# Attention values in plain float32: one matmul in place of three, one copy in place of a split

## The chip, the cores and the metric

The kernel runs as one program on one core of a Trainium2 chip. Its time is the device time in microseconds of that core. Three runs of the kernel before gave 996.60, 995.01 and 995.56 us, a median of 995.56. A further execution was taken with the hardware profiler; all the rows below are from it.

## The reference, cut to what matters

The reference is one encoder layer on 512 tokens of width 1024, in float32: a half-step gated feed-forward network, a mixing block with two groups of eight attention heads, a second half-step feed-forward network and a final norm. The change touches the mixing block alone:

```
qa, ka = rmsnorm(...), rmsnorm(...)          # group A: 8 heads of 64
va = proj[..., o_va:o_cq]
p  = softmax(qa ka^T * scale + bias, masked) # 64-token chunks, block-causal
out_a = p @ va
...
q, k = [nope 64 | rotary 32]                 # group B: 8 heads, 96 wide
v  = kv[..., B_NOPE:]
p  = softmax(q k^T * scale, masked)
out_b = p @ v
x = x + concat(out_a, out_b) @ w_out
```

With 512 tokens, each 128-query block sees the keys up to its own block, so of the 4 x 4 blocks of a head's probabilities ten are computed.

## The kernel before, in words

Everything is kept transposed or split so that the tensor engine (PE) does nearly all the work. A float32 operand is split in two float32r parts, a high part (a rounding copy, mostly on the scalar engine, ACT) and a low part (what is left, on the vector engine, DVE, or on GpSimd, POOL). A product is then three float32r matmuls: high x high, high x low, low x high. The helper `mm3` at lines 146 to 149 issues them, so in the profile L147, L148 and L149 are the three products of every matrix multiply, and the tiles' names tell which one it is. Weights come in units of up to 1024 columns through `wunit` (L139 load, L142 high part, L143 low part) with four buffers each for the raw, high and low tiles (tags `raw`, `whi`, `wlo`).

The stages follow each other in time: first feed-forward network (up to about 362 us), the mixing block (362 to 579 us), output projection (`wo`, from 579 us) and the second feed-forward network. The order of instructions on each engine is set by a scheduler when the program is built, from the order of the code and its own estimates, and each engine then runs its queue in that order. Only the very end has an order written out by hand.

In the mixing block `in_proj` gives A's queries, keys and values; the latents give B's queries (`uq`) and B's keys and values (`ukv`, L414). B's values are evacuated from `ukv` into VBh and VBl (L426, L427). GpSimd squares B's keys (`sqk`, L420), DVE sums them (`ssk`), and their norm factors (`f_kn`) follow. It also applies B's rotary embedding to the queries (lines 294 to 304). A's keys need their own norm factors: squares on ACT (`sqp`, L330), sums on DVE (`ss_ka`, L331), the reciprocal root (`f_ka`, lines 114 to 119 and 288), and a multiply (kA, L375). A's values come last (`values_proj`, VAh and VAl). The value tiles are 192 columns wide for each pair of heads: values of the even head, 64 zeros, values of the odd head. A 128-column window of it as the stationary operand puts one head in its half of the output rows and adds zeros to the other half, so a pair of heads accumulates into one bank `pv`.

The loop over 16 heads runs four steps on different heads: `front` makes the transposed query and key operands, `softmax` makes the four row blocks of probabilities (scores `s`, minimum and mask on DVE at L522, exponential on ACT at L524, reciprocal on DVE, scaling on GpSimd at L526), `flip` transposes the ten 128 x 128 blocks on PE into three banks t0, t1, t2 (L542) and copies them out, and `values` multiplies them with the values into `pv`. Heads 0 to 7 are group A, with a contraction of 64 rows in the scores; heads 8 to 15 are group B, with 96 rows.

In `flip`, the transposed probabilities for keys in block 0, 1, 2 and 3 have 512, 384, 256 and 128 query columns. Block 3 is widened with 128 zero columns to 256 (the GpSimd memsets at L544). Each of the four pieces is copied as a high part by ACT (L547), then DVE subtracts that from the bank for the low part (L548). `values` then issues four times three matmuls, with 512, 384, 256 and 256 columns.

Of the kernel before, what the change touches and what calls it, by code (L numbers as in the profile page):

```python
# [10 lines left out]
F32 = mybir.dt.float32  # L11
F32R = mybir.dt.float32r
# [5 lines left out]
P = 128  # L18
# [21 lines left out]
def tile_macaron_block(  # L40
# [207 lines left out]
    with tc.tile_pool(name="mix", bufs=1, side="left", reuse_waits="tile") as mp:  # L248
        latT = mp.tile([P, 6, S], F32R, tag="vAh", name="latT")
        VBh = mp.tile([P, NT, 4, 192], F32R, tag="vBh", name="VBh")  # L250
        qA = mp.tile([P, NT, 512], F32, tag="qA", name="qA")
        VBl = mp.tile([P, NT, 4, 192], F32R, tag="vBl", name="VBl")
# [4 lines left out]
        for t in (VBh, VBl):  # L257
            pool.memset(t[:, :, :, HD:2 * HD].bitcast(F32), 0.0)
# [47 lines left out]
        with tc.tile_pool(name="ps2", bufs=1, space=PSUM, reuse_waits="tile") as ps:  # L306
# [102 lines left out]
            for t in range(NT):  # L409
                tt = slice(t * P, (t + 1) * P)  # L410
                for half in range(2):
# [10 lines left out]
                    for e in range(2):  # L422
                        vh = VBh[:, t, 2 * half:2 * half + 2, 2 * HD * e:2 * HD * e + HD]
                        vl = VBl[:, t, 2 * half:2 * half + 2, 2 * HD * e:2 * HD * e + HD]
                        src = pv[:, e::2, HD:2 * HD]
                        act.copy(vh, src)  # L426
                        dve.tensor_tensor(out=vl, in0=src, in1=vh.bitcast(F32), op=ALU.subtract)  # L427
# [8 lines left out]
            def values_proj():  # L436

                VAh = mp.tile([P, NT, 4, 192], F32R, tag="vAh", name="VAh")
                VAl = mp.tile([P, NT, 4, 192], F32R, tag="vAl", name="VAl")
                for t in (VAh, VAl):  # L440
                    pool.memset(t[:, :, :, HD:2 * HD].bitcast(F32), 0.0)
                pts = in_proj(416 + 1024, 512, 1)
                for t in range(NT):
                    pv = pts[t].rearrange("p (h e w) -> p h e w", e=2, w=HD)
                    for e in range(2):
                        vh = VAh[:, t, :, 2 * HD * e:2 * HD * e + HD]
                        vl = VAl[:, t, :, 2 * HD * e:2 * HD * e + HD]
                        act.activation(vh, pv[:, :, e, :], AF.Copy, scale=rtok[:, t:t + 1])
                        dve.scalar_tensor_tensor(out=vl, in0=pv[:, :, e, :], scalar=rtok[:, t:t + 1], in1=vh.bitcast(F32),
                                                 op0=ALU.mult, op1=ALU.subtract)  # L450
                return VAh, VAl
# [77 lines left out]
            def flip(pi):  # L529
# [4 lines left out]
                PAh = wpool.tile([P, 1024], F32R, tag="whi", name="PAh")  # L534
                PAl = wpool.tile([P, 1024], F32R, tag="wlo", name="PAl")
                PBh = wpool.tile([P, 1024], F32R, tag="whi", name="PBh")
# [204 lines left out]
```

## Time and profile before

| what | value |
|---|---|
| median of three runs | 995.56 us |
| time of the profiled execution | 997.57 us |
| its span | 995.8 us |
| mean granted PE clock | 0.994 of full speed |
| PE busy | 975.5 us, 98% of the span |
| DVE, ACT, POOL busy | 390.5, 391.9, 579.6 us |
| the 16 heads | about 473 to 579 us |

The profiled execution took 997.57 us, of which 995.8 lie between its first and its last instruction; the remaining 1.8 us are around it. A busy time is the sum over the stretch in which an engine had an instruction running. Matmuls are pipelined: the next starts before the one before has ended, so a record's length (0.39 us for 512 columns) is longer than the distance from one start to the next, and the distance is what a matmul costs in a dense stream.

### The profile page before, as it was taken

Reading aid. Unit: us, or ns where it says so; the run is one execution under the profiler, and the core shown is the slowest. Engines: PE = TensorE matmul, PEld = TensorE weight load, DVE = VectorE, ACT = ScalarE, POOL = GpSimd, SP = SyncE. Lnnn points to the kernel's source line nnn. Section 1 sums busy time; section 2 is a strip of 40 time slices with the busy share of each in tenths; the row PEclk is TensorE's granted clock in tenths of the full one; section 3 lists DMA queues with packets and bytes.
Section 4 is the critical chain, followed back from the end, with each engine's and each line's share of the span. In section 5 each row is a group of like instructions: output and inputs, shape, how many; then the busy total and the mean of one; then the engine's idle time right before and its main releaser. Section 6 shows DMA issues by size and latency. Waiting matters only on the chain.

```text
span 995.8 us, 12076 instructions
## 1 busy us (share of the span) xinstructions
PE 975.5 (98%) x4579; PEld 812.1 (82%) x4579; DVE 390.5 (39%) x684; ACT 391.9 (39%) x661; POOL 579.6 (58%) x424
## 2 busy tenths in 40 slices
PE   9999999999999999898999999999999999999996
PEld 6888888888888889786778978888888888888886
DVE  7533333333121233866788845143333333200002
ACT  7533323232222236563778853343233232322321
POOL 4776666765555530385445567587666667645541
PEclk9999999999999999999999999999999999999998
DMA  6432223233233242220110062323322232333302
GB/s 233 145 109 86 102 89 106 85 106 95 83 102 93 89 141 75 85 64 1 32 33 2 1 212 88 103 86 106 102 88 99 93 104 80 101 96 95 101 16 85
DMA packets 29146, 89.90 MB, mean 90 GB/s; under 512 B 3488, under 2 KB 5664, under 8 KB 29088
## 3 DMA queue, kind: packets, MB, share of 16 engines
q1 hardware_dynamic: 28224, 88.34, 27.6%
q8 instruction: 36, 0.59, 0.2%
q10 hardware_dynamic: 864, 0.79, 0.2%
q14 instruction: 22, 0.18, 0.1%
HBM read 87.02 MB, written 2.10 MB: 89 GB/s over the span
## 4 chain that ended last, share of the span: by engine, by line
PE 89%; DVE 4%; ACT 3%; POOL 2%; issue 1%; DMA 1%; SPq 0%; POOLq 0%; ACTq 0%; DVEq 0%
PE gu L147 15%; PE gu L149 15%; PE gu L148 15%; PE dn L147 8%; PE dn L149 8%; PE dn L148 8%; PE pj L149 2%; PE pj L147 2%; PE pj L148 2%; PE wo L147 1%; PE wo L149 1%; PE wo L148 1%; PE t L542 1%; PE s L147 1%; PE tr L457 1%
## 5 line engine op out<-in xcount | busy, mean ns | idle before, releaser
L143 POOL TENSOR_TENSOR wlo<-raw,whi 128x1024 fp32r<-128x1024 f32 x138 | 324.2, 2350 | 153.3 <-ACT whi L142 152.5
L142 ACT CAST whi<-raw 128x1024 fp32r<-128x1024 f32 (+2 forms) x159 | 162.4, 1022 | 447.7 <-PE gu L148 244.8
L147 PE MATMUL gu<-x2h,whi 128*128 128x512 f32 x352 | 136.9, 389 | 0.0
L148 PE MATMUL gu<-x2l,whi 128*128 128x512 f32 x352 | 136.8, 389 | 0.0
L149 PE MATMUL gu<-x2h,wlo 128*128 128x512 f32 x352 | 136.8, 389 | 0.0
L148 PE MATMUL gu<-xl,whi 128*128 128x512 f32 x320 | 124.5, 389 | 0.0
L147 PE MATMUL gu<-xh,whi 128*128 128x512 f32 x320 | 124.5, 389 | 0.0
L149 PE MATMUL gu<-xh,wlo 128*128 128x512 f32 x320 | 124.5, 389 | 0.0
L162 POOL TENSOR_TENSOR us<-us,gs 128x512 f32<-128x512 f32 x44 | 57.6, 1310 | 108.7 <-DVE us L160 107.2
L161 DVE SCALAR_TENSOR_TENSOR gs<-th,gs 128x512 f32<-128x512 f32 x44 | 91.1, 2074 | 31.8 <-ACT th L159 31.8
L158 DVE TENSOR_TENSOR gs<-gu,rs 128x512 f32<-128x512 f32 x44 | 30.4, 691 | 175.9 <-PE gu L149 168.7
L191 DVE SCALAR_TENSOR_TENSOR x<-dn,x 128x512 f32<-128x512 f32 (+1 forms) x17 | 11.2, 660 | 193.9 <-PE dn L149 193.9
L148 PEld LDWEIGHTS gu<-x2l,whi 128*128 128x128 f32 x352 | 66.1, 188 | 13.8
L149 PEld LDWEIGHTS gu<-x2h,wlo 128*128 128x128 f32 x352 | 66.1, 188 | 13.8
L147 PEld LDWEIGHTS gu<-x2h,whi 128*128 128x128 f32 x352 | 66.1, 188 | 13.6
L149 PEld LDWEIGHTS gu<-xh,wlo 128*128 128x128 f32 x320 | 60.1, 188 | 12.6
L147 PEld LDWEIGHTS gu<-xh,whi 128*128 128x128 f32 x320 | 60.1, 188 | 12.5
L148 PEld LDWEIGHTS gu<-xl,whi 128*128 128x128 f32 x320 | 60.1, 188 | 12.3
L147 PE MATMUL dn<-h1h,whi 128*128 128x512 f32 x176 | 68.5, 389 | 0.0
L148 PE MATMUL dn<-h1l,whi 128*128 128x512 f32 x176 | 68.5, 389 | 0.0
L149 PE MATMUL dn<-h1h,wlo 128*128 128x512 f32 x176 | 68.5, 389 | 0.0
L160 DVE SCALAR_TENSOR_TENSOR us<-gu,rs 128x512 f32<-128x512 f32 x44 | 30.4, 690 | 64.9 <-PE gu L149 64.9
(327 smaller groups left out, 1864.5 us busy)
## 6 DMA issues: line engine op xcount, KB each, us to landing
raw<-in_gu SPq DMA_DIRECT2D x84, 512.0 KB, 3.6
raw<-in_dn SPq DMA_DIRECT2D x32, 512.0 KB, 3.5
raw<-in_dn SPq DMA_DIRECT2D x16, 384.0 KB, 3.1
raw<-in_w_in SPq DMA_DIRECT2D x12, 512.0 KB, 3.4
raw<-in_w_out SPq DMA_DIRECT2D x8, 512.0 KB, 4.3
x<-in_xT SPq DMA_DIRECT2D x8, 256.0 KB, 5.4
raw<-in_gu SPq DMA_DIRECT2D x8, 256.0 KB, 5.4
bias<-in_bias_tab SPq DMA_DIRECT2D x8, 256.0 KB, 2.7
```

The costliest lines, as they stand in the source:

```text
L142: act.copy(hi[:, :n], raw[:, :n])
L143: (lo_on or pool).tensor_tensor(out=lo[:, :n], in0=raw[:, :n], in1=hi[:, :n].bitcast(F32), op=ALU.subtract)
L147: pe.matmul(out, lhsT=ah, rhs=bh, start=start, stop=False)
L148: pe.matmul(out, lhsT=ah, rhs=bl, start=False, stop=False)
L149: pe.matmul(out, lhsT=al, rhs=bh, start=False, stop=stop)
L158: dve.tensor_tensor(out=gs, in0=gup[0], in1=rs, op=ALU.mult)
L160: dve.scalar_tensor_tensor(out=us, in0=gup[1], scalar=0.5, in1=rs, op0=ALU.mult, op1=ALU.mult)
L161: dve.scalar_tensor_tensor(out=gs, in0=th, scalar=1.0, in1=gs, op0=ALU.add, op1=ALU.mult)
L162: pool.tensor_tensor(out=us, in0=us, in1=gs, op=ALU.mult)
L191: dve.scalar_tensor_tensor(out=x[dt][:, h], in0=pt[:, h], scalar=0.5, in1=x[dt][:, h], op0=ALU.mult, op1=ALU.add)
L457: pe.transpose(pt[0:src(t).shape[1], t * P:(t + 1) * P], src(t), ident)
L542: pe.transpose(tt[:, o + i * P:o + (i + 1) * P], pi[i][:, j * P:(j + 1) * P], ident)
```

## The change

The probabilities and the values are no longer split. The value tiles VB and VA and the copied probabilities PA and PB are plain float32, and `values` issues one plain float32 matmul for each of the four key blocks, with 512, 384, 256 and 128 columns. The piece for key block 3 now lies beside that for block 2 in bank t2, and there are no zero columns. Three copies take the place of four copies and four subtractions: DVE copies t2 and t1 (384 columns each), ACT copies t0 (512). Of the values, each eviction is one copy, on DVE for even heads and on ACT for odd ones. The memsets of the low tiles and of the zero columns are gone. Scores, projections, the output projection and both feed-forward networks keep their three float32r products, and `pv` is still split into AH and AL for the output projection.

```
@@ -247,15 +247,13 @@
     AH, AL = XH, XL
     with tc.tile_pool(name="mix", bufs=1, side="left", reuse_waits="tile") as mp:
         latT = mp.tile([P, 6, S], F32R, tag="vAh", name="latT")
-        VBh = mp.tile([P, NT, 4, 192], F32R, tag="vBh", name="VBh")
+        VB = mp.tile([P, NT, 4, 192], F32, tag="vBh", name="VB")
         qA = mp.tile([P, NT, 512], F32, tag="qA", name="qA")
-        VBl = mp.tile([P, NT, 4, 192], F32R, tag="vBl", name="VBl")
         kA = mp.tile([P, NT, 512], F32, tag="kA", name="kA")
         lat = mp.tile([P, NT, LAT], F32, tag="qB", name="lat")
         kB = mp.tile([P, NT, 512], F32, tag="kB", name="kB")
         kpe = mp.tile([P, NT, QK], F32, tag="kpe", name="kpe")
-        for t in (VBh, VBl):
-            pool.memset(t[:, :, :, HD:2 * HD].bitcast(F32), 0.0)
+        pool.memset(VB[:, :, :, HD:2 * HD], 0.0)
         pool.memset(kpe, 0.0)
         ctab = mp.tile([P, NT, 2, 16], F32, tag="ctab", name="ctab")
         nc.sync.dma_start(out=ctab, in_=rope_tab)
@@ -420,11 +418,8 @@
                     pool.tensor_tensor(out=sq, in0=kv, in1=kv, op=ALU.mult)
                     dve.tensor_reduce(out=ssk[:, t, hs], in_=sq, op=ALU.add, axis=AX.X)
                     for e in range(2):
-                        vh = VBh[:, t, 2 * half:2 * half + 2, 2 * HD * e:2 * HD * e + HD]
-                        vl = VBl[:, t, 2 * half:2 * half + 2, 2 * HD * e:2 * HD * e + HD]
-                        src = pv[:, e::2, HD:2 * HD]
-                        act.copy(vh, src)
-                        dve.tensor_tensor(out=vl, in0=src, in1=vh.bitcast(F32), op=ALU.subtract)
+                        dst = VB[:, t, 2 * half:2 * half + 2, 2 * HD * e:2 * HD * e + HD]
+                        (act.copy if e else dve.tensor_copy)(out=dst, in_=pv[:, e::2, HD:2 * HD])
             fk = factors(ssk, NH, HD, False, "kn")
             for t in range(NT):
                 dv = kB[:, t, :].rearrange("p (h w) -> p h w", w=HD)
@@ -435,20 +430,18 @@
 
             def values_proj():
 
-                VAh = mp.tile([P, NT, 4, 192], F32R, tag="vAh", name="VAh")
-                VAl = mp.tile([P, NT, 4, 192], F32R, tag="vAl", name="VAl")
-                for t in (VAh, VAl):
-                    pool.memset(t[:, :, :, HD:2 * HD].bitcast(F32), 0.0)
+                VA = mp.tile([P, NT, 4, 192], F32, tag="vAh", name="VA")
+                pool.memset(VA[:, :, :, HD:2 * HD], 0.0)
                 pts = in_proj(416 + 1024, 512, 1)
                 for t in range(NT):
                     pv = pts[t].rearrange("p (h e w) -> p h e w", e=2, w=HD)
                     for e in range(2):
-                        vh = VAh[:, t, :, 2 * HD * e:2 * HD * e + HD]
-                        vl = VAl[:, t, :, 2 * HD * e:2 * HD * e + HD]
-                        act.activation(vh, pv[:, :, e, :], AF.Copy, scale=rtok[:, t:t + 1])
-                        dve.scalar_tensor_tensor(out=vl, in0=pv[:, :, e, :], scalar=rtok[:, t:t + 1], in1=vh.bitcast(F32),
-                                                 op0=ALU.mult, op1=ALU.subtract)
-                return VAh, VAl
+                        dst = VA[:, t, :, 2 * HD * e:2 * HD * e + HD]
+                        if e:
+                            act.activation(dst, pv[:, :, e, :], AF.Copy, scale=rtok[:, t:t + 1])
+                        else:
+                            dve.tensor_scalar(out=dst, in0=pv[:, :, e, :], scalar1=rtok[:, t:t + 1], scalar2=None, op0=ALU.mult)
+                return VA
 
             def transposes(src):
 
@@ -531,32 +524,25 @@
                 t0 = ps.tile([P, 512], F32, tag="t", name="t0", bufs=NB["t"])
                 t1 = ps.tile([P, 512], F32, tag="t", name="t1", bufs=NB["t"])
                 t2 = ps.tile([P, 512], F32, tag="t", name="t2", bufs=NB["t"])
-                PAh = wpool.tile([P, 1024], F32R, tag="whi", name="PAh")
-                PAl = wpool.tile([P, 1024], F32R, tag="wlo", name="PAl")
-                PBh = wpool.tile([P, 1024], F32R, tag="whi", name="PBh")
-                PBl = wpool.tile([P, 1024], F32R, tag="wlo", name="PBl")
-                where = {0: (t0, 0), 1: (t1, -128), 2: (t2, -256), 3: (t2, 0)}
+                PA = wpool.tile([P, 1024], F32, tag="whi", name="PA")
+                PB = wpool.tile([P, 1024], F32, tag="wlo", name="PB")
+                where = {0: (t0, 0), 1: (t1, -128), 2: (t2, -256), 3: (t2, -128)}
                 for i in (3, 2, 1, 0):
                     for j in range(i + 1):
                         tt, o = where[j]
                         pe.transpose(tt[:, o + i * P:o + (i + 1) * P], pi[i][:, j * P:(j + 1) * P], ident)
-                for hl in (PBh, PBl):
-                    pool.memset(hl[:, 256:384].bitcast(F32), 0.0)
-                for h_, l_, src in ((PBh[:, 384:512], PBl[:, 384:512], t2[:, 384:512]), (PBh[:, 0:256], PBl[:, 0:256], t2[:, 0:256]),
-                                    (PAh[:, 512:896], PAl[:, 512:896], t1[:, 0:384]), (PAh[:, 0:512], PAl[:, 0:512], t0)):
-                    act.copy(h_, src)
-                    dve.tensor_tensor(out=l_, in0=src, in1=h_.bitcast(F32), op=ALU.subtract)
-                return [(PAh[:, 0:512], PAl[:, 0:512], 0), (PAh[:, 512:896], PAl[:, 512:896], 128),
-                        (PBh[:, 0:256], PBl[:, 0:256], 256), (PBh[:, 256:512], PBl[:, 256:512], 256)]
+                dve.tensor_copy(out=PB[:, 0:384], in_=t2[:, 0:384])
+                dve.tensor_copy(out=PA[:, 512:896], in_=t1[:, 0:384])
+                act.copy(PA[:, 0:512], t0)
+                return [(PA[:, 0:512], 0), (PA[:, 512:896], 128), (PB[:, 0:256], 256), (PB[:, 256:384], 384)]
 
             def values(h, seg):
                 if h % 2 == 0:
                     shared["pv"] = ps.tile([P, 512], F32, tag="pv", name="pv", bufs=NB["pv"])
                 pv, e, pr = shared["pv"], h % 2, (h % NH) // 2
-                Vh, Vl = shared["V"] if h < NH else (VBh, VBl)
-                vc = slice(HD * e, HD * e + P)
-                for j, (ph, pl, q0) in enumerate(seg):
-                    mm3(pv[:, q0:S], Vh[:, j, pr, vc], Vl[:, j, pr, vc], ph, pl, e == 0 and j == 0, e == 1 and j == NT - 1)
+                V = shared["V"] if h < NH else VB
+                for j, (p, q0) in enumerate(seg):
+                    pe.matmul(pv[:, q0:S], lhsT=V[:, j, pr, HD * e:HD * e + P], rhs=p, start=e == 0 and j == 0, stop=e == 1 and j == NT - 1)
                 if e == 1:
                     c = h // 2
                     act.copy(AH[c], pv)
```

The scheduler also orders the queues of the mixing block anew. The first place is PE's queue at the end of the last head: in its rows `t` is a bank of transposed probabilities, pa and pb are the probabilities, pv the result of a head pair, and wo the output projection. Before:

```order
L148 MATMUL pv<-PAl,VBh 128x512
L149 MATMUL pv<-PAh,VBl 128x512
L147 MATMUL pv<-PAh,VBh 128x384
L148 MATMUL pv<-PAl,VBh 128x384
L149 MATMUL pv<-PAh,VBl 128x384
L147 MATMUL pv<-PBh,VBh 128x256
L148 MATMUL pv<-PBl,VBh 128x256
L149 MATMUL pv<-PBh,VBl 128x256
L147 MATMUL pv<-PBh,VBh 128x256
L148 MATMUL pv<-PBl,VBh 128x256
L149 MATMUL pv<-PBh,VBl 128x256
L147 MATMUL wo<-xh_81,whi 128x512
```

Now:

```order
L533 MATMUL t_4669<-ident,pb 128x128
L533 MATMUL t_4670<-ident,pb 128x128
L545 MATMUL pv<-PA,VB 128x512
L545 MATMUL pv<-PA,VB 128x384
L545 MATMUL pv<-PB,VB 128x256
L545 MATMUL pv<-PB,VB 128x128
L533 MATMUL t_4669<-ident,pb 128x128
L545 MATMUL pv<-PA,VB 128x512
L545 MATMUL pv<-PA,VB 128x384
L545 MATMUL pv<-PB,VB 128x256
L545 MATMUL pv<-PB,VB 128x128
L147 MATMUL wo<-xh_81,whi 128x512
```

Twelve matmuls of the last head have become four, and one transpose of the last head (of its first query block, into t0) now stands after the products of the head before and directly ahead of the last four products.

The second place is DVE's queue between the norm factors of B's keys (f_kn) and those of A's keys (f_ka); sqp are the squares of A's keys and ss_ka their sums, wlo the low part of a weight unit. Before:

```order
L285 TENSOR_SCALAR f_kn<-ssk 128x32
L143 TENSOR_TENSOR wlo<-raw,whi 128x1024
L116 TENSOR_TENSOR z_kn<-y_kn 128x32
L117 TENSOR_TENSOR z_kn<-z_kn,f_kn 128x32
L118 TENSOR_SCALAR z_kn<-z_kn 128x32
L119 TENSOR_TENSOR f_kn<-y_kn,z_kn 128x32
L331 TENSOR_REDUCE ss_ka<-sqp 128x8 x3
L143 TENSOR_TENSOR wlo<-raw,whi 128x1024
L331 TENSOR_REDUCE ss_ka<-sqp 128x8
L282 TENSOR_TENSOR f_ka<-ss_ka,vtok 128x32
L283 TENSOR_SCALAR f_ka<-f_ka 128x32
```

Now:

```order
L283 TENSOR_SCALAR f_kn<-ssk 128x32
L329 TENSOR_REDUCE ss_ka<-sqp 128x8
L116 TENSOR_TENSOR z_kn<-y_kn 128x32
L329 TENSOR_REDUCE ss_ka<-sqp 128x8
L117 TENSOR_TENSOR z_kn<-z_kn,f_kn 128x32
L329 TENSOR_REDUCE ss_ka<-sqp 128x8
L118 TENSOR_SCALAR z_kn<-z_kn 128x32
L119 TENSOR_TENSOR f_kn<-y_kn,z_kn 128x32
L143 TENSOR_TENSOR wlo<-raw,whi 128x1024
L329 TENSOR_REDUCE ss_ka<-sqp 128x8
L280 TENSOR_TENSOR f_ka<-ss_ka,vtok 128x32
L281 TENSOR_SCALAR f_ka<-f_ka 128x32
```

Three of the four sums of A's keys now stand between the steps of f_kn, where before they stood behind all of them.

GpSimd's queue moves at the same place: five squares of B's keys stand behind the scaling of B's queries where four did, and one step of the rotary embedding (L301 before, L299 now) stands ahead of the last of them.

## Rows read from the trace of the kernel before

**Rows 1.** The page: busy time, and the chain by engine.

```profile
PE 975.5 (98%) x4579; PEld 812.1 (82%) x4579; DVE 390.5 (39%) x684; ACT 391.9 (39%) x661; POOL 579.6 (58%) x424
...
PE 89%; DVE 4%; ACT 3%; POOL 2%; issue 1%; DMA 1%; SPq 0%; POOLq 0%; ACTq 0%; DVEq 0%
```

**Rows 2.** Busy time by engine in three stretches; PEclk is the granted clock.

```profile
core 0: us, PE busy (x) PEld busy (x) DVE busy (x) ACT busy (x) POOL busy (x), PEclk, DMA share, GB/s
460.00:480.00 20.00, 15.81 (x70) 12.44 (x69) 9.16 (x22) 6.83 (x14) 3.78 (x6) 0.91 0.00 0
480.00:580.00 100.00, 98.05 (x629) 81.54 (x628) 83.83 (x292) 80.23 (x227) 52.35 (x102) 1.00 0.12 38
987.00:990.00 3.00, 1.22 (x2) 0.50 (x2) 1.75 (x7) 0.77 (x2) 0.53 (x2) 0.54 0.80 264
```

**Rows 3.** Timeline of the tensor engine, last head: start us, us, instruction, count.

```profile
576.46 0.40 PE L147 MATMUL pv<-PAh,VBh 128*128 128x512 f32 x1
...
577.16 0.34 PE L147 MATMUL pv<-PAh,VBh 128*128 128x384 f32 x1
...
577.51 0.34 PE L149 MATMUL pv<-PAh,VBl 128*128 128x384 f32 x1
578.15 0.38 PE L147 MATMUL pv<-PBh,VBh 128*128 128x256 f32 x1 [0.30 <-ACT PBh L547]
578.61 0.39 PE L148 MATMUL pv<-PBl,VBh 128*128 128x256 f32 x1
```

**Rows 4.** The same timeline near the end, around a plain float32 matmul.

```profile
983.18 0.28 PE L148 MATMUL dn<-xl,whi 128*128 128x256 f32 x1
983.30 0.60 PE L639 MATMUL rb<-dg,one 128*128 128x256 f32 x2
983.54 0.47 PE L149 MATMUL dn<-xh,wlo 128*128 128x256 f32 x1
983.85 0.28 PE L147 MATMUL dn<-xh,whi 128*128 128x256 f32 x1
```

**Rows 5.** The same timeline in an A head, around a block of transposes.

```profile
523.80 0.28 PE L149 MATMUL s<-xh,xl 64*128 64x256 f32 x1
524.01 0.55 PE L542 MATMUL t<-ident,pa 128*128 128x128 f32 x3
524.31 0.47 PE L148 MATMUL pv<-PAl,VAh 128*128 128x512 f32 x1
524.62 0.39 PE L149 MATMUL pv<-PAh,VAl 128*128 128x512 f32 x1
```

**Rows 6.** The same in a B head, around a block of transposes.

```profile
575.42 0.28 PE L147 MATMUL pv<-PBh,VBh 128*128 128x256 f32 x1
575.54 0.49 PE L542 MATMUL t<-ident,pa 128*128 128x128 f32 x3
...
575.99 0.28 PE L149 MATMUL pv<-PBh,VBl 128*128 128x256 f32 x1
```

**Rows 7.** Line 548: count, ns least/median/most, first and last start.

```profile
L548 DVE TENSOR_TENSOR PBl<-t,PBh x32: 265/344/425, 486.5 to 578.1; 128x128 fp32r<-128x128 f32 x16, 128x256 fp32r<-128x256 f32 x16
L548 DVE TENSOR_TENSOR PAl<-t,PAh x32: 528/615/692, 487.6 to 574.8; 128x384 fp32r<-128x384 f32 x16, 128x512 fp32r<-128x512 f32 x16
```

**Rows 8.** Waits of the tensor engine, 480 to 572 us: total us, times, longest.

```profile
PE s L147 <- DVE mn L522: 0.8, 2, 0.4
```

**Rows 9.** Timeline of GpSimd: the last square of keys, then rotary work.

```profile
448.39 0.62 POOL L420 TENSOR_TENSOR sqk<-kB 128x256 f32<-128x256 f32 x1
448.96 1.29 POOL L301 TENSOR_TENSOR qB<-rtmp 128x512 f32<-128x512 f32 x1
```

**Rows 10.** Timeline from the key projection of A to its transposes.

```profile
455.01 0.60 ACT L330 ACTIVATE sqp<-pj 128x512 f32<-128x512 f32 x1 [1.94 <-PE pj L149]
...
463.66 2.48 DVE L375 TENSOR_TENSOR kA<-pj,f_ka 128x512 f32<-128x512 f32 x4
...
465.70 1.08 PE L457 MATMUL tr<-ident,qA 128*128 128x128 f32 x4 [4.19 <-DVE kA L375]
```

## The prediction

> **What bounds the kernel now.** I read the page first: PE is busy for 98% of the span, and 89% of the chain that ended last is PE's [rows 1]. So the question is what the change does to PE's queue in the mixing block, and whether any other engine takes over there. Next come the stretches: from 480 to 580 us, where the heads run, PE is busy 98.05 of 100 us, DVE 83.83, ACT 80.23 [rows 2]. A busy PE can still be a PE that runs loosely, so the third view is its timeline, where the distance from one start to the next tells the cost. In a dense run three products of 512 columns take 577.16 - 576.46 = 0.70, so 0.233 each, and two of 384 columns 577.51 - 577.16 = 0.35, so 0.175 each [rows 3]; one of 256 columns takes 983.30 - 983.18 = 0.12 [rows 4]. That is proportional to the columns but for some 0.015 us each. In a B head a block of three transposes between two products adds nothing beyond its own 0.109 per transpose: 575.42 + 0.12 + 3 x 0.109 + 0.12 = 575.99, as the rows have it [rows 6]. PE is streaming without a hole. In an A head the same sum from 523.80 gives 523.80 + 0.12 + 0.33 + 0.233 = 524.48, and the row stands at 524.62 [rows 5]: 0.14 is lost where 64-row score products and 128-row work meet. Real waits of PE on others in the heads are small: 0.8 us in two waits for DVE to empty a score bank [rows 8]. The largest hole lies ahead of the heads: 4.19 us until A's keys are normalised [rows 10], with a granted clock of 0.91 over 460 to 480 [rows 2].
>
> **The products.** Before, a head's values take 3 x 0.233 + 3 x 0.175 + 6 x 0.12 = 1.94 us of stream. Afterwards they are 512 + 384 + 256 + 128 = 1280 columns of plain float32. The trace has one such product in a dense run, the 256 columns of rb, recorded as two instructions: from its start at 983.30 to 983.85 there lie rb and one 256-column float32r product, so rb costs 0.55 - 0.12 = 0.43 us, or 1.68 ns a column [rows 4]. That makes 2.15 us a head, 0.21 more than now, and 16 x 0.21 = +3.3 us. A second rb, alone, took 1.22 us in a stretch with a granted clock of 0.54 [rows 2], near the lower of its two levels (1.2 and 2.4 GHz); 4.8 ns a column would mean 67 us more. The float32 transposes take 0.109 per 128 columns [rows 6], or 0.85 ns a column, and would mean 14 us less. The dense rb is the same operation amid the same neighbours at full clock, so I take it and hold the other two for excluded, the one by its clock, the other because a transpose is not a product. What I keep as a bound is the hand-over: if each of the eight records of a head cost the 0.015 us of a float32r product, 16 x 8 x 0.015 = 1.9 us come on top.
>
> **Boundaries in the A heads.** Counted in PE's queue, 49 places where 64-row score products meet other work become 43. At 0.14 each [rows 5] that is -0.9 us; none at all, or twice that price, are the ends (0 to -1.7).
>
> **DVE and ACT.** The four subtractions of a head cost 2 x 0.344 + 2 x 0.615 = 1.92 us by their medians [rows 7]; two copies of 384 columns cost about 2 x 0.53 by the shortest of PAl's records, that of the same width. DVE thus loses some 0.86 us a head, 13.8 us in all, and ACT three of its four copies. In the heads this is off the path, because PE has no hole there: it can give back at most the 0.8 us of waits [rows 8]. I take -0.4. The evictions of the values and the memsets lie beside PE's projections; they act only by way of the queues of the next part.
>
> **The hole ahead of the heads.** PE's transposes of A's queries and keys use score and transpose banks that kA must leave first. From the end of the last sqk at 449.01 [rows 9] the path runs over f_kn, the sums of squares of A's keys, f_ka and kA (463.66 and 2.48 long) to 465.70 [rows 10], 16.7 us. The new queues move it both ways. On GpSimd one rotary step of 1.29 [rows 9] now stands ahead of the last sqk, and one sqk of 0.62 that was done while it waited now comes after; against that the low parts are gone from DVE's queue ahead of B's query factors, worth about 1.1, so sqk ends some 0.8 later. On DVE three of A's four sums no longer stand behind all of f_kn, so ACT's wait of 1.94 for a square's buffer [rows 10] goes. I take 0.8 - 1.9 = -1.1 us. The ends are +1.9 (1.29 + 0.62, and nothing saved) and -4.2 (the hole is gone). What is late next, if it shrinks, is again kA. The clock: 0.91 over 20 us is 1.8 us of missing pulses, part of them in the hole itself. A shorter hole may spare some; I take -0.5, with 0 and -1.5 as ends.
>
> **The end of the last head.** Now PE stands at 577.51 + 0.175 = 577.69 until 578.15, and 0.34 more until 578.61, for the high and low copies of t2 [rows 3], 0.8 in all. Afterwards the last transpose goes to t0 directly ahead of the last four products, which must wait for its travel and ACT's copy of 512 columns: of the size of the longest record of line 548, 0.69 [rows 7], less what hides the transpose. The output projection is queued behind it. I take -0.3, with +0.5 and -0.8 as ends.
>
> **Sum.** 3.3 - 0.9 - 0.4 - 0.3 - 1.1 - 0.5 = +0.1 us on a profiled execution of 997.57 us, 1.8 of it outside the span. That execution was 2.0 over the median of 995.56, so I forecast 995.6 us: no change. A difference of 0.2% (2 us) is about what can be told from no change here.
>
> **A rule that speaks against this.** From 480 to 580 the weight loads of PE are busy 81.54 us and DVE 83.83 [rows 2]. The Trainium skill, "Perfetto Trace Analysis", section "Identifying the Most-Contended Engine", says that matmul busy time is no good measure of PE's headroom, that the busy share of the weight loads should be used, and that the engine with the highest occupancy binds. By that rule DVE would be the bound of the heads, and its 13.8 us would come off. The distances in the B heads say otherwise: nothing is left between the products for DVE to give back [rows 6].
>
> **Rivals.** First, DVE sets the pace of the heads: 16 x 0.86 = -13.8 us, 981.8 us. For it speaks DVE's share, against it the streaming above. Second, the same price for the products, but the hole goes whole: +3.3 - 0.9 - 0.8 - 0.8 - 4.2 - 1.5 = -4.9, about 990.7 us. For it speaks that four evictions' worth of DVE and ACT work leaves the queues ahead of kA; against it that GpSimd's queue stays in that path. Third, on the other side: the plain float32 stream is dearer than any saving. Each record pays the hand-over (+1.9), the A boundaries give nothing, and the late sqk lengthens the hole by 1.9 with the clock as it is: 3.3 + 1.9 + 1.9 - 0.4 - 0.3 = +6.4, about 1002 us. It decides once f_kn is so late that ACT's squares wait longer than the 1.94 they wait now; with the hand-over alone, and the hole unchanged, the time would be near 999.
>
> **Chances.** Forecast 0.61, the hole goes 0.20, dearer stream 0.15, DVE's pace 0.04. Of the forecast's own case about a seventh lies beyond 2 us, two thirds of it on the faster side; the first two rivals are faster nearly always, the third nearly always slower. So faster 0.29, same 0.54, slower 0.17. The range that should hold the time 8 times in 10 reaches well into the second case and to the milder form of the third: 991.0 to 999.2.
>
> **What will show it.** In the profile after, pv products of 512 columns should come as pairs of records with 0.85 us from one product to the next, a head's four taking about 2.15; 2.25 and more would mean the hand-over. DVE's busy time over the heads should fall by some 14 us with the stretch no shorter by more than 2; if the stretch falls with it, PE did not bind. PE's wait for kA should be about 3 us; zero makes the second rival, 5 or more the third. The granted clock of the 20 us around it should be between 0.91 and 1.00. I am wrong at the root if the heads' stretch changes by more than 5 us in either direction.

## The result, and the profile after

| kernel | median us (lowest to highest, runs) | against before, 95% |
|---|---|---|
| before, beside the first comparison | 996.15 (995.01 to 996.98, 5) | 1 |
| after | 1001.52 (1000.03 to 1003.07, 5) | 1.0051 [1.0039, 1.0062] |
| after, repeated on another occasion | 1001.00 (1000.27 to 1005.48, 6) | 1.0055 [1.0036, 1.0074] |

The change makes the kernel slower by 0.5%, some 5.3 us, where no change was forecast; the range ended at 999.2. The profiled execution is the one of 1003.07 us, the slowest of its five and 1.5 us above their median.

The page's busy times and its chain by engine, which answer to [rows 1]:

```profile
PE 978.7 (98%) x4515; PEld 806.6 (81%) x4515; DVE 376.5 (38%) x640; ACT 376.0 (38%) x601; POOL 572.6 (57%) x390
...
PE 88%; DVE 3%; POOL 2%; issue 2%; DMA 2%; ACT 2%; SPq 0%; POOLq 0%; DVEq 0%; ACTq 0%
```

The page alone hides the result: PE is busy 98% as before. The stretches of [rows 2], with their columns:

```profile
460.00:480.00 20.00, 17.04 (x77) 12.66 (x76) 9.79 (x25) 5.56 (x13) 2.18 (x3) 0.91 0.00 0
480.00:580.00 100.00, 96.75 (x542) 72.98 (x540) 71.14 (x252) 63.56 (x171) 47.74 (x72) 0.98 0.11 33
```

DVE lost 12.7 us and ACT 16.7 in the heads' 100 us, and PE waits more, not less. From the first score product to the first product of the output projection PE took 106.06 us before (473.24 to 579.30 in its timeline) and takes 113.17 now (471.26 to 584.43): +7.1 us. The rest of the span is 1.6 us shorter. The four places that matter follow in PE's timeline.

First, the products of a B head, against [rows 3, 6]:

```profile
552.72 1.67 PE L545 MATMUL pv<-PA,VB 128*128 128x512 f32 x4
554.23 0.82 PE L545 MATMUL pv<-PB,VB 128*128 128x256 f32 x4
554.88 0.49 PE L533 MATMUL t<-ident,pa 128*128 128x128 f32 x3
```

A plain product is recorded as two instructions, and a row takes adjoining ones of the same tiles together: its x4 are two of 512 and two of 384 columns. From the first product to what follows the fourth: 554.88 - 552.72 = 2.16 us, eight records without a gap. Second, the end of the last head, against the last two rows of [rows 3]:

```profile
578.55 0.27 PE L533 MATMUL t<-ident,pb 128*128 128x128 f32 x1
582.26 1.77 PE L545 MATMUL pv<-PA,VB 128*128 128x512 f32 x4 [3.43 <-ACT PA L536]
583.86 0.82 PE L545 MATMUL pv<-PB,VB 128*128 128x256 f32 x4
584.43 0.48 PE L147 MATMUL wo<-xh,whi 128*128 128x512 f32 x1
```

PE stands 3.43 us for the copy of t0, with the output projection queued behind it; before, it stood 0.8 us in two pieces, for the copies of t2. ACT's timeline at the end of the last head, first before:

```profile
573.71 0.97 ACT L547 CAST PAh<-t 128x384 fp32r<-128x384 f32 x2
575.66 1.05 ACT L142 CAST whi<-raw 128x1024 fp32r<-128x1024 f32 x1 [0.99 <-PE pv L149]
...
576.77 1.05 ACT L142 CAST whi<-raw 128x1024 fp32r<-128x1024 f32 x1
577.73 0.37 ACT L547 CAST PBh<-t 128x256 fp32r<-128x256 f32 x1
```

Now:

```profile
575.96 1.03 ACT L142 CAST whi<-raw 128x1024 fp32r<-128x1024 f32 x1
577.86 1.05 ACT L142 CAST whi<-raw 128x1024 fp32r<-128x1024 f32 x1 [0.87 <-DMA raw<-in_w_out]
580.67 1.04 ACT L142 CAST whi<-raw 128x1024 fp32r<-128x1024 f32 x1 [1.76 <-DMA raw<-in_w_out]
581.62 0.58 ACT L536 COPY PA<-t 128x512 f32<-128x512 f32 x1
```

The bank was complete at about 578.8. The copy takes 0.58 us, but it stands in ACT's queue behind two casts of the output projection's weights, and the second of them waits for its transfer until 580.67. Before, the copy of t0 (the second of the pair at 573.71) went ahead of the casts, and only the small copies of t2 stood between them: the wait that ended at 578.15 was for the one at 577.73, itself behind a cast. Third, PE at the start of the heads:

```profile
486.23 0.44 PE L147 MATMUL s<-xh,xh 64*128 64x384 f32 x1 [0.47 <-DVE mn L515]
...
487.95 0.55 PE L533 MATMUL t<-ident,pa 128*128 128x128 f32 x3 [0.46 <-ACT PA L536]
...
488.64 1.92 PE L545 MATMUL pv<-PA,VA 128*128 128x512 f32 x2
```

and the granted clock there, microsecond by microsecond (the columns of [rows 2]):

```profile
487.00:488.00 1.00, 0.54 (x5) 0.31 (x4) 0.97 (x4) 0.69 (x2) 0.60 (x2) 1.00 0.43 125
488.00:489.00 1.00, 1.00 (x6) 0.98 (x7) 0.05 (x1) 1.00 (x3) 0.00 (x0) 0.72 0.36 137
489.00:490.00 1.00, 1.00 (x2) 0.34 (x1) 1.00 (x3) 0.20 (x2) 0.14 (x1) 0.50 0.00 0
490.00:491.00 1.00, 1.00 (x3) 0.35 (x2) 0.44 (x3) 0.00 (x0) 0.48 (x1) 0.50 0.00 0
491.00:492.00 1.00, 1.00 (x4) 0.67 (x3) 0.00 (x0) 0.00 (x0) 1.00 (x2) 0.57 0.00 0
```

After two waits of nearly half a microsecond the first products run at 0.50, the lower of the two levels; before, the same microseconds read 1.00. PE is busy throughout, so by these rows the fall costs 0.28 + 0.50 + 0.50 + 0.43 = 1.7 us (an estimate). Fourth, the hole ahead of the heads, against [rows 10]:

```profile
463.33 0.63 PE L450 MATMUL tr<-ident,qA 128*128 128x128 f32 x4 [2.96 <-DVE kA L373]
```

It is 1.23 us shorter. In e1, whose PE queue is the same, it is 2.37, so one profile tells it to within about half a microsecond. What PE waits for in the heads otherwise has grown a little; these rows answer to [rows 8] (the columns are total us, times, longest), with 0.4 for a fourth score bank at 566.8 us on top:

```profile
PE s L147 <- DVE mn L515: 0.9, 2, 0.5
PE t L533 <- ACT PA L536: 0.5, 1, 0.5
PE t L533 <- POOL pa L519: 0.3, 1, 0.3
```

### The profile page after: what moved, and what is told of

The parts are those of the page before. It is cut to its first block, busy times and chain, and to the rows that moved or that the text cites. A ratio compares the mean times of both kernels' runs of the same rounds, so it can differ in the third digit from the quotient of the medians.

```text
span 1001.3 us, 11789 instructions
## 1 busy us (share of the span) xinstructions
PE 978.7 (98%) x4515; PEld 806.6 (81%) x4515; DVE 376.5 (38%) x640; ACT 376.0 (38%) x601; POOL 572.6 (57%) x390
## 4 chain that ended last, share of the span: by engine, by line
PE 88%; DVE 3%; POOL 2%; issue 2%; DMA 2%; ACT 2%; SPq 0%; POOLq 0%; DVEq 0%; ACTq 0%
PE gu L148 15%; PE gu L147 15%; PE gu L149 15%; PE dn L147 8%; PE dn L149 8%; PE dn L148 8%; PE pv L545 3%; PE pj L147 2%; PE pj L148 2%; PE pj L149 2%; PE t L533 1%; PE wo L148 1%; PE wo L149 1%; PE wo L147 1%; PE s L147 1%
## 5 line engine op out<-in xcount | busy, mean ns | idle before, releaser
L147 PEld LDWEIGHTS gu<-x2h,whi 128*128 128x128 f32 x352 | 66.1, 188 | 13.8
L148 PEld LDWEIGHTS gu<-x2l,whi 128*128 128x128 f32 x352 | 66.1, 188 | 13.8
L519 POOL TENSOR_TENSOR pa<-pa,sm 128x512 f32<-128x512 f32 (+1 forms) x32 | 30.0, 940 | 51.6 <-DVE sm L518 50.1
```

The lines of the kernel that those rows point to most:

```text
L147: pe.matmul(out, lhsT=ah, rhs=bh, start=start, stop=False)
L148: pe.matmul(out, lhsT=ah, rhs=bl, start=False, stop=False)
L519: pool.tensor_tensor(out=pi[i], in0=pi[i], in1=sm[:, i:i + 1].broadcast_to([P, (i + 1) * P]), op=ALU.mult)
```

## The experiments

The runs edit the kernel after, but for e4, e6 and e7, which edit the kernel before. Each ran against the kernel before on the same chip. All medians, with the granted clock of the single runs (mean over the span):

| run | median us | ratio to before, 95% | clock of its runs |
|---|---|---|---|
| before, beside four sets (9 to 26 runs each) | 996.33 to 996.73 | 1 | 0.991 to 0.995 |
| after, both occasions | 1001.52, 1001.00 | see above | 0.990 to 0.994 |
| e1 last copy on DVE | 999.74 | 1.0037 [1.0025, 1.0050] | 0.989 to 0.992 |
| e2 all t0 copies on DVE | 999.22 | 1.0027 [1.0018, 1.0035] | 0.992 to 0.997 |
| e3 one rounded product | 987.33 | 0.9895 [0.9871, 0.9920] | 0.982 to 0.992 |
| e4 block 3 plain | 996.81 | 1.0007 [0.9999, 1.0016] | 0.991 to 0.994 |
| e5 first transposes later | 993.18 | 0.9969 [0.9959, 0.9979] | 0.995 to 0.997 |
| e6 the same on before | 997.68 | 1.0014 [1.0003, 1.0025] | 0.990 to 0.994 |
| e7 e4 and last copy on DVE | 994.54 | 0.9983 [0.9975, 0.9992] | 0.992 to 0.995 |
| e8 filled waits | 1000.77 | 1.0040 [1.0027, 1.0052] | 0.993 to 0.996 |
| e9 plain in eight heads | 993.21 | 0.9962 [0.9949, 0.9976] | 0.994 to 0.997 |
| e10 dead subtractions | 998.57 | 1.0027 [1.0017, 1.0037] | 0.992 to 0.996 |
| e11 e8 and last copy on DVE | 1001.06 | 1.0050 [1.0038, 1.0063] | 0.995 to 0.996 |

The scheduler builds each edited kernel anew. By the traces PE's instructions come in the same order in after, its repeat and e1, and in e4 and e7. In all the others some instructions of the heads have changed places as well, so that a time there belongs to the edit and its new order together.

**The end of the last head (e1, the repeat, e2).**

```diff
-                act.copy(PA[:, 0:512], t0)
+                (dve.tensor_copy if last else act.copy)(out=PA[:, 0:512], in_=t0)
```

> The changed kernel with one instruction moved: in the last head alone, the copy of the bank t0 of transposed probabilities (PA[:, 0:512] <- t0, 0.58 us) goes to DVE and not ACT. Theory (the wait of 3.43 us of PE before the last head's first product is this copy standing in ACT's queue behind two casts of w_out, which wait for their transfers): the wait falls to 0.5 to 1 us, since DVE is free there, and the time is 2.4 to 3.0 us under the changed kernel's, about 998.8 us; the heads otherwise as they were. Rival (the last head's probabilities or transposes are themselves late, so the copy's engine doesn't matter): wait and time unchanged, about 1001.5 us. The plain products' +3.4 us over the heads remains in either case, so that the kernel stays above the one before by about 2.5 us.

PE's and DVE's timelines of e1:

```profile
577.50 0.27 PE L533 MATMUL t<-ident,pb 128*128 128x128 f32 x1
578.55 1.77 PE L545 MATMUL pv<-PA,VB 128*128 128x512 f32 x4 [0.78 <-DVE PA L536]
```

```profile
577.81 0.69 DVE L536 COPY PA<-t 128x512 f32<-128x512 f32 x1 [1.70 <-PE t L533]
```

The wait fell from 3.43 to 0.78 us, as the theory has it: the transposes were ready, ACT's queue was not. The rival is out. The median fell by 1.3 to 1.8 us, less than the 2.4 to 3.0 expected from this one profile; its span fell by 3.9 (1001.3 to 997.4), but the first profile is of the slowest run.

> The changed kernel itself, unedited, beside the others of this call, to compare the tail's edit with it on one chip. If its time is again near 1001.5 us, the edit of the last copy (999.74 us) is worth about 1.8 us; its profile should show the wait of PE of 3 to 3.6 us before the last head's first product again. Open is the clock: if the half clock at 488 to 492 us (after PE's waits of 0.47 and 0.46 us) is there again it belongs to the change; if the clock is 1.00 there, it came by chance in the first profile, and the time is about 1 to 2 us lower.

The repeat shows the wait again, at 2.70 us, since it hangs on when the weights land; against that one e1 saves 1.9 us of wait, and the span is 1.9 shorter (999.3 to 997.4). The half clock was there again, after the same two waits (0.47 and 0.46 us), and costs the same 1.7 us; it begins earlier, so that it reads 0.66 over 485 to 490 us and 1.00 over 490 to 495.

With all 16 copies on DVE:

> The changed kernel with the copy of the bank t0 of transposed probabilities on DVE in all 16 heads (ACT has none of the three). Theory 1 (the end of the last head waits for ACT's queue, and the half clock at 488 to 492 us follows PE's waits of 0.46 to 0.47 us at 486 to 488 us, one of which is for this copy on ACT): the tail's wait falls by 2.4 to 3.0 us as in the run with the last copy alone; if the copy on DVE also comes 0.4 us earlier at 488 us and the clock then stays at 1.00, another 1.7 us goes: 997.1 us. If the clock falls nevertheless, 998.8 us. Rival (DVE, 71 us busy of 100 in the heads, then sets when the score banks come free): 16 copies x 0.6 us = 9.6 us more on DVE, waits of PE for mn grow by 0.3 us or more for each head, about 1003 us or above.

At 999.22 us it is no better than e1 beyond their spread, and DVE did not become the bound: the waits for mn did not grow. At the end PE waited 0.76 and 1.14 us, as DVE now copies t1 and t0 one after the other. Its profiled execution, the fastest of 11 at 997.22, kept a clock of 1.00 through the mixing block, although PE waited 0.47 and 0.32 us at 484 to 486, and came out near the 997.1 expected for that case. The other ten have a mean clock of 0.992 to 0.995, so that this profile does not stand for them.

**The price of the product (e3).** Probabilities, values and their copies are declared in the rounded form.

> The changed kernel with probabilities and values in the rounded 32-bit matmul form: one product of high parts for each key block, the low parts left out of the computation; all copies, transposes and their engines as in the changed kernel. It prices the plain product by itself. Theory (TensorE bounds the heads, and each product's columns are on the path at 2.16 us a head): a rounded product of 512, 384, 256 and 128 columns takes some 0.23 + 0.18 + 0.12 + 0.12 (estimate for the last: as the 256) = 0.65 us, so the heads are shorter by up to 16 x 1.5 = 24 us: 977 to 980 us, with the tail's wait of 3.4 us still there. Rival (the chain of score, softmax on DVE/ACT/POOL and transposes sets a head's time, and the plain product only fills time that PE would wait): the heads shorten by less than a third of that, 994 us or more, and PE's waits for mn and PA grow by as much as the products shrink.

PE's timeline of e3 in an A head, and its clock:

```profile
534.53 0.65 PE L545 MATMUL pv<-PA,VA 128*128 128x512 f32 x2
535.02 0.34 PE L545 MATMUL pv<-PB,VA 128*128 128x256 f32 x2
535.20 0.60 PE L450 MATMUL tr<-ident,kB 128*64 128x128 f32 x4
```

```profile
490.00:495.00 5.00, 5.00 (x14) 3.14 (x13) 2.17 (x9) 1.46 (x4) 2.13 (x4) 0.50 0.00 0
495.00:500.00 5.00, 5.00 (x20) 4.18 (x19) 1.87 (x9) 2.12 (x7) 1.46 (x2) 0.50 0.18 52
```

Four products take 0.67 us (535.20 - 534.53) where the plain ones take 2.16, and the heads 98.07 us where they took 113.17. That is 15.1 and not 24 in this execution, which spent the 10 us shown at half clock, and more after them: 10.2 us lost over 488 to 509 us, by the granted clock. The two runs at a clock of 0.990 and 0.992 took 980.8 and 982.2 us, the four at 0.982 to 0.984 took 987.0 to 989.3. PE's products are on the path: the rival wanted 994 or more.

**A cheaper mixture, given back at the end (e4, e7).** In e4 the last key block alone is plain:

```diff
+                    if pl is None:
+                        pe.matmul(pv[:, q0:S], lhsT=V3["A" if h < NH else "B"][:, pr, vc], rhs=ph, start=False, stop=e == 1)
+                        continue
```

> The kernel before with only the last key block (128 queries) as a plain product: its values in a tile of their own, its probabilities copied once by DVE; the three other blocks stay split into three rounded products. Theory (a product costs what PE's start-to-start times say: plain 1.68 ns a column against three rounded products of 256 columns at 0.12 us, so that the plain form is dearer from 256 columns up and cheaper at 128): 16 x (0.36 - 0.22) = 2.2 us less of PE, with one ACT copy, one DVE subtraction and two memsets of POOL fewer for each head, about 994 us against 996.2. Rival (the switch between plain and rounded products, or the weight load of the plain one, costs more than the difference of columns): 996 to 998 us. Rival 2 (PE's half clock early in the heads comes with any shorter work on DVE and ACT): the clock at 486 to 492 us under 0.8, time 996 us.

No gain: the first rival's time, though not for its reason. ACT's and PE's timelines of e4 at the end of the last head:

```profile
573.91 0.49 ACT L556 CAST PAh<-t 128x384 fp32r<-128x384 f32 x1
574.29 2.08 ACT L142 CAST whi<-raw 128x1024 fp32r<-128x1024 f32 x2
576.27 0.58 ACT L556 CAST PAh<-t 128x512 fp32r<-128x512 f32 x1
```

```profile
576.90 0.50 PE L147 MATMUL pv<-PAh,VBh 128*128 128x512 f32 x1 [2.01 <-ACT PAh L556]
```

Two casts stand ahead of the copy of the same bank: the product's saving was spent on a wait of 2.01 us. In this execution, the slowest of 11, the clock then fell to 0.50 at 578 to 580 us, which costs 1.7 us more. e7 gives that one copy to DVE:

> The kernel with only the last key block plain (split for the others), and in the last head the high part of the bank t0 copied by DVE and not ACT. Theory (the 2.2 us saved in PE's products were given back at the end of the last head, where PE waited 2.01 us for this copy behind two casts of w_out in ACT's queue): the wait falls to about 0.8 us, time 1.2 to 1.5 us less than the 996.8 us of the kernel without this edit: about 995.4 us, under the kernel before. Rival (the saved time went into the waits of 0.24 to 0.41 us in the heads, and the tail's wait only moves to the DVE subtraction that follows): no change, 996.5 us or more.

The wait fell to 0.78 us, the half clock after it is missing, and the time fell by 2.3, more than expected, to 994.54: 0.17% under before. The shape is the one that the prediction's own price favours (0.36 against 0.22 us for 128 columns), but the 2.2 us that this price promises are not shown to be the ones gained: in the profiles the heads are 0.95 us shorter than before (105.11 against 106.06), with 0.96 us more of waits.

**The order ahead of the heads (e5, e6, e10).** e5 is e1 with A's first transposes behind 14 more matmuls of the value projection:

```diff
-                with (tc.high_priority(offset=150) if it < 1 else ExitStack()):
+                with (tc.high_priority(offset=150 if it > -2 else 40) if it < 1 else ExitStack()):
```

> The changed kernel with the last copy on DVE and, besides, the transposes of the first head pair (tr <- qA, kA) issued 14 instructions of the value projection later on PE, so that PE has that projection to do while kA is being scaled. Theory (PE's wait of 2.4 to 3 us for kA ahead of the heads and the half clock that follows it are a matter of order only; a PE that never waits there keeps 1.00): the wait goes, the clock at 465 to 470 us is 1.00 and not 0.7 to 0.88, 3.5 to 4 us less than with the last copy alone: about 996 us. The clock at 485 to 492 us then shows whether the second dip needs the first. Rival (the first head's chain of score, softmax and transposes has then 3 us less of projection to hide it, and PE waits there instead): the wait reappears between 472 and 488 us, time about 999.5 us.

> The kernel before with the first head pair's transposes issued 17 instructions of the value projection later on PE, as in the run on the changed kernel. Theory (the wait of 4.19 us for kA is order only): 4 us less and the clock at 465 to 470 us at 1.00 and not 0.66, about 991 us. Rival (the wait moves to the first head's softmax): about 996 us.

The clock of e5 where the hole and the second dip were:

```profile
460.00:465.00 5.00, 5.00 (x26) 3.97 (x25) 3.44 (x9) 0.52 (x2) 0.69 (x1) 1.00 0.00 0
465.00:470.00 5.00, 5.00 (x26) 4.07 (x25) 1.99 (x3) 1.41 (x3) 0.00 (x0) 1.00 0.00 0
...
485.00:490.00 5.00, 5.00 (x30) 3.56 (x29) 3.62 (x11) 2.13 (x7) 2.40 (x4) 1.00 0.00 0
```

The hole is gone, and so are the waits at 485 to 488 and both dips: 993.18 us, 6.6 under e1 and faster than before. In the profiles e1's hole of 2.37 us, its two dips of 1.7 each and 0.6 of waits in the heads come to 6.4, and the spans differ by 6.1. A third dip of e1, at 410 to 415 us, cost nothing: PE then misses the wait of 1.24 us that it has at 418 us in after, and goes on at the same time. The expectation had left the second dip open; it is 1.7 of the 2.8 us by which the time came out under 996.

On the kernel before, the same move (with 45 for 40, 17 matmuls) gained nothing, 997.68 us. PE's timeline of e6, at the start of the heads and at the end of the last, and its clock:

```profile
483.56 0.53 PE L542 MATMUL t<-ident,pa 128*128 128x128 f32 x2 [1.28 <-DVE PAl L548]
...
577.85 0.50 PE L147 MATMUL pv<-PAh,VBh 128*128 128x512 f32 x1 [1.76 <-ACT PAh L547]
```

```profile
485.00:490.00 5.00, 5.00 (x18) 3.92 (x17) 2.65 (x11) 1.99 (x9) 1.59 (x3) 0.50 0.15 46
```

One wait moved to a subtraction of the split, and the clock fell after it, as the rival has it. But at the end a second one came: the copy of t0 now stands behind two weight casts, as in after, and e6 lacks the edit of the last copy that e5 has. So e5 and e6 differ by more than the splits. e10 tests the splits on e5 itself, by giving it the removed work back as dead work:

```diff
+                    (dve.tensor_copy if last and w == 512 else act.copy)(out=d, in_=src[:, 0:w])
+                    dve.tensor_tensor(out=junk[:, 0:w], in0=src[:, 0:w], in1=d, op=ALU.subtract)
```

> The plain kernel with the last copy on DVE and the first transposes 14 instructions later (993.2 us), and on top the work on ACT and DVE that the change removed, put back as dead work: all three copies of transposed probabilities on ACT (t0 of the last head on DVE), followed by a subtraction on DVE of the same size into a tile that nothing reads; likewise for the values of the first eight heads. PE's instructions are the same; the first transposes stand at the same place behind 355 matmuls of the projections. Theory (the later transposes pay in the plain kernel and not in the kernel before because the first heads' chain on ACT and DVE is short enough only without the splits): PE waits again for 1 us or more between 480 and 490 us, with the clock at 0.5 after it, and in the heads at several places: 996 to 1000 us. Rival (the kernel before got nothing from the later transposes because of its own order of split products): no such wait, 993 to 994.5 us.

998.57 us, 5.4 over e5. The first transposes stand where they stand in e5, but later in the heads the scheduler has put PE's instructions in another order. PE's timeline of e10, and its clock:

```profile
483.76 0.44 PE L147 MATMUL s<-xh,xh 64*128 64x384 f32 x1 [0.39 <-DVE mn L515]
```

```profile
485.00:490.00 5.00, 5.00 (x11) 2.96 (x12) 2.71 (x11) 2.23 (x7) 2.80 (x5) 0.50 0.15 47
```

The waits are shorter than expected (0.34 at 478 us, 0.39 here, and 0.90 at 500 us), but the clock fell all the same. In this execution, at 1002.04 us the slowest of ten, the heads are 7.7 us longer than in e5: 3.4 by the clock, 1.1 by waits, and 3.2 that neither accounts for. So the removed work on ACT and DVE costs about 5 us when it is put back here; how much of that is PE's new order was not shown by itself.

**The half clock (e8, e11).**

```diff
+                        for _ in range(fill):
+                            pe.transpose(shared["pv"][:, 0:P], pi[i][:, j * P:(j + 1) * P], ident)
```

> The changed kernel with 20 extra transposes on PE (each of the second head's ten transposes is done twice more, into the bank of the values' products before their first product; nothing reads them). At 0.109 us each they are 2.2 us, of which about 0.9 us stand in PE's waits of 0.47 and 0.46 us at 485 to 488 us. Nothing else is moved. Theory (the half clock of the first values' products follows these waits of PE): the clock from 485 to 495 us is 1.00 in the profile, and the time is 1.2 us of extra transposes less 1.7 us of clock, 0 to 1 us under the changed kernel's 1001.3. Rival (the clock falls there for another reason, such as the earlier dip at 465 to 470 us or the plain products themselves): the dip is there again, and the time is 1.2 us or more above, about 1002.5 us.

> The kernel with 20 extra transposes in PE's waits at 485 to 488 us, and the last head's t0 copy on DVE. In the profile of the extra transposes alone the clock was 1.00 both after the wait for kA (465 to 470 us, where nothing was edited) and at 485 to 495 us, so that it does not tell whether the second dip goes because its waits are filled or because the first dip was missing. Theory (filled waits keep the clock): if the clock after the wait for kA is below 1.00 here, it is nevertheless 1.00 from 485 to 495 us. Rival (the second dip comes with the first): both below 1.00, or both 1.00 again, which would leave it open. Time: the tail's edit on top, 1.5 to 2.7 us less than 1000.8 us: 998.1 to 999.3 us.

The clock of e8 after the hole, where nothing was edited, and where the waits were filled:

```profile
465.00:470.00 5.00, 5.00 (x24) 3.71 (x22) 0.61 (x1) 0.00 (x0) 0.00 (x0) 1.00 0.00 0
...
485.00:490.00 5.00, 5.00 (x31) 3.59 (x30) 3.13 (x14) 3.22 (x9) 2.47 (x6) 1.00 0.19 52
```

Both dips are missing, in e11 as well, so these runs do not tell whether the second goes because its waits are filled; e11's case for settling it did not arise. Other profiles answer a part of it: the second dip does not need the first (e6 and e10 read 1.00 over 465 to 470 us), nor does the first bring the second (before, e4 and e7 read 0.66, 0.67 and 0.73 there and 1.00 over 485 to 495). The time of e8 stays near that of after, as the theory had it: 2.2 us of extra transposes, partly in waits, against the clock. e11 missed its expected time by 1.8 to 3 us; with its wait at the end falling only from 1.70 to 1.14 us the edit had little to take.

**A mixture of heads (e9).**

> A mixture: the first eight heads (A) as in the changed kernel, with plain products; the last eight (B) with three rounded products for the key blocks of 512, 384 and 256 columns and a plain one for 128 columns; the last head's t0 high part copied by DVE; the first head pair's transposes 14 instructions of the value projection later. Theory (with PE never waiting ahead of the heads the kernel is bound by PE's stream, and a split block of 256 columns or more is cheaper there: 8 heads x 0.35 us = 2.8 us less than the 993.2 us of the plain kernel with the two moves; the relief of ACT and DVE is needed only where the first head's chain is uncovered): 990.5 us. Rival (in the last eight heads the splits on ACT and DVE bring back waits of 0.2 to 0.4 us, as in the kernel with only the last block plain): 992.5 to 994 us, no better than the plain one.

PE's timeline of e9, ahead of the heads and behind them:

```profile
465.33 0.30 PE L460 MATMUL tr<-ident,qA 128*128 128x128 f32 x1 [1.06 <-DVE kA L377]
...
575.30 0.51 PE L149 MATMUL wo<-xh,wlo 128*128 128x512 f32 x1 [0.78 <-POOL wlo L143]
```

The heads took 100.94 us against 103.74 in e5, 2.8 less as expected, but the kernel is no faster: 1.06 us came back as a hole before the first transposes and 0.78 as a wait of the output projection for its low weights. The rival's time was right, its place (the last eight heads) was not.

## Why the prediction was wrong

By the prediction's own sign it was wrong at the root: the heads' stretch changed by 7.1 us, more than 5. By its steps, on the profiled executions (995.8 to 1001.3 us of span, +5.5 where +0.1 was forecast):

- The products: +3.3 forecast, 16 x (2.16 - 1.94) = +3.5 measured. No hand-over between records. Right, and e3 shows that the products are on the path.
- The hole: -1.1 forecast, -1.23 measured. The way is the forecast one, with luck in the sum: against the rest of the program, which ran 1.14 us earlier on PE, the last square of B's keys ended 1.6 us later and not 0.8, and the path from there to the transposes took 13.9 us for 16.7, 2.8 less and not 1.9. Its clock: -0.5 forecast, nothing measured (0.91 in both).
- **The end of the last head: -0.3 forecast, with +0.5 and -0.8 as ends; +2.6 measured (3.43 less 0.8). This is the step that failed**, in size and in its bounds. It priced the copy that PE would wait for (0.69 us) and not what stands ahead of it in ACT's queue: two weight casts, one of them waiting for a transfer. e1, and e7 against e4, show it, with PE's order unchanged. The step is not the whole miss: with it mended e1 still takes 999.74 us, 3.3 over before and above the range.
- The clock in the heads: put at nothing, without a reason; +1.7 measured, in both profiles of after and in e1. That it follows the waits at 484 to 488 us is what these profiles, e3, e6 and e10 have in common; it was not shown by itself, and why PE waits there now was not tested.
- DVE's waits: -0.4 forecast. Apart from the end, PE's waits in the heads grew by 0.5 (1.55 to 2.06, all over 0.05 us). DVE did lose 12.7 of the 13.8 us, and as argued that gave no time: the first rival, DVE's pace, is out for this order. So is the rule of the Trainium skill, "Perfetto Trace Analysis", section "Identifying the Most-Contended Engine", that the prediction sets against itself: DVE, the engine with the higher share, was relieved, and nothing came off. e3, where PE's shorter products saved 15.1 us in the heads, speaks the same way.
- Boundaries in the A heads: -0.9 forecast; what the other terms leave of the heads' +7.1 is 7.1 - 3.5 - 2.6 - 1.7 - 0.5 = -1.2, inside the ends but not measured by itself.

The third rival named the time, 1002 us, by luck, for reasons that did not occur: eight records of a head take 2.16 us and not the 2.27 of the hand-over, and the wait for kA shrank.

## What to carry to other kernels

Price a new wait by the queue of the engine that serves it, not by the instruction alone: at a stage's last step the next stage's preparations may already stand ahead of it, waiting for transfers. Work taken from engines that are not the bound may pay only after the bound's own order lets it: here it brought nothing as it stood, while with PE's first transposes behind work that it could do meanwhile, the same work put back cost about 5 us (e5 against e10, PE's order in the heads differing too). And compare a cheaper instruction shape by shape: the plain product loses at 512 columns (0.86 against 0.70 us from start to start) and wins at 128 (0.22 against 0.36, as the split form is widened to 256 columns).

## What the hardware showed that was not expected

- In after, its repeat, e1 and e3 PE waited 0.47 and 0.46 us at the start of the heads and then ran at half clock, which cost 1.7 us (10.2 in e3); in e10 the waits were 0.34 and 0.39 us and the cost 3.4. In e2, with waits of 0.47 and 0.32 us, the clock stayed at 1.00.
- A wait of 3.0 us for kA, behind the same PE instructions, was followed by half clock in after, its repeat and e3 (as was one of 2.37 us in e1), and by 1.00 in e2, e8 and e11. Each of these falls cost 1.7 us; that they read 0.70 to 0.89 over 465 to 470 us comes from where they lie in that stretch. What decides is open.
- At the end of the last head, waits of 2.01 us in e4 and 1.76 in e6 were followed by half clock, and those of 3.43 us in after, 2.70 in its repeat and 1.70 in e8 were not. This too is open.
- The rounded single product of e3, which left PE waiting more often, spent 490 to 505 us at 0.50 and 505 to 510 at 0.63: a good part of what the shorter stream saved was lost to the clock.
